# One five-bank PSUM tile for the scores of two attention units, one maximum and one exponential per unit

## The chip, the cores and the metric

The kernel runs on one core of a Trainium2 chip. The metric is the device time of one execution in microseconds, as the median of several runs.

## The reference

A two-layer backbone over 1024 latent tokens and 256 context tokens with a model width of 1024. Each layer normalises its input, makes one combined projection, feeds three groups of heads (gated DeltaNet, latent attention, GLA), gates them and makes one output projection. Context reads only context, latent tokens read all 1280. The change touches the attention of the latent head group:

```python
def attend(q, k, v):
    s = jnp.einsum('bqhd,bkhd->bhqk', q, k).astype(jnp.float32) * MLA_SCALE
    p = jax.nn.softmax(s, axis=-1).astype(v.dtype)
    return jnp.einsum('bhqk,bkhd->bqhd', p, v)

o_l = blocked_attention(q_l, concat([k_c, k_l]), concat([v_c, v_l]))   # 8 heads, 1024 queries, 1280 keys
o_c = attend(mla_q(cq_c, ...), k_c, v_c)                               # 256 queries, 256 keys, first layer only
```

## The kernel before, in words

Each layer runs in stages: projections, preparation of the DeltaNet, the up-projections of attention (`up`, L1014), attention (`attend`, L1134) and the output projection. The two recurrent scans run in the background: `background` (L1453) is a generator that goes through the DeltaNet scan (`gdn_scan`, 20 steps, two or three yields each), then the GLA preparation, seven GLA levels (`gla_level`) and the GLA scan. `up` takes its first 28 steps. In `run`, the loop at L1481 calls the background's next step after each yield of `attend`, so yields fix how the two are mixed in the order of the program. The framework turns that into a fixed order of instructions for each engine, which need not be the program's, and puts in the waits.

`attend` goes through units. A unit is one head and 128 queries (at i < CT, 256 context queries against 256 keys, done as two halves of 128). Two heads `hh` and two query tiles make a group of four units, and four pairs of heads `m` make 64 units of the large kind in each layer, and 8 of the context kind in the first. A unit goes through these steps:

- `first(u, c0)` (L1190) makes the scores of the keys 0 to 511 and 512 to 1023 into `sa`, a tile of two PSUM banks with two buffers. Each piece is three matmuls (`mm3`, L253 to L257, from high and low halves of queries and keys). After the second piece VectorE takes the negated maximum over 1024 keys (L1206).
- `second(u)` (L1208) makes the scores of the last 256 keys into half of `sb`, a tile of one bank that two following units share (L1222 to L1224), takes their maximum (L1225), the smaller of the two negated maxima (L1226), and then two exponentials on ScalarE with that bias, 256 keys from `sb` (L1227) and 1024 from `sa` (L1228), each with a sum into `rd`. They write the tile `P`, which has three buffers.
- `transposed(u, ka)` (L1230) turns P in pieces of 128 keys on TensorE, four to a bank of the tag `t` (two buffers), and copies them to `PT`: the first and last piece on ScalarE, the middle one on VectorE (L1247).
- `output(m, i)` (L1250) runs once for the four units of a group: 20 pairs of value and PT through TensorE into the tile `O` (L1255), the two sums added (L1261) and inverted (L1262), a diagonal of them multiplied in (L1267), and the gate (L1269, L1271).

The loop from L1278 sets the order of the program. In step u it issues `second(u)`, then three times a part of `transposed(u - 1)` and, at the first two of them, a part of `first(u + 1)`, with a yield after each, and `output` where a group has ended. That makes six yields a unit, and one more for an output. PSUM is full: `sa` 4 banks, `sb` 1, `t` 2, and 1 for the background (tag `l`).

Of the kernel before, what the change touches and what calls it, by code (L numbers as in the profile page):

```python
# [9 lines left out]
F32 = mybir.dt.float32  # L10
F32R = mybir.dt.float32r
U32 = mybir.dt.uint32
AF = mybir.ActivationFunctionType
ALU = mybir.AluOpType
AX = mybir.AxisListType
# [4 lines left out]
T = 1280  # L20
CT = 2
# [22 lines left out]
class Net:  # L44
# [1089 lines left out]
    def attend(self, l, fill=None):  # L1134
        nc, sp = self.nc, self.ap
        last = l == L - 1
        mm = nc.tensor.matmul
        V, A, P = nc.vector, nc.scalar, nc.gpsimd
# [34 lines left out]
        sb, mxs, sas, ps, PT, rds = {}, {}, {}, {}, {}, {}  # L1173
# [16 lines left out]
        def first(u, c0):  # L1190

            m, i, hh = units[u]
            if i < CT:
                if c0 == 0:
                    sas[u] = sa = self.ps.tile([128, 1024], F32, name="sa", tag="sa", bufs=2)[:, 0:512]
                    for j in range(2):
                        scores(u, sa[:, 256 * j:256 * j + 256], 0, 256, j)
                    mxs[u] = mx = sp.tile([128, 2], F32, name="mx", tag="mx", bufs=4)
                    V.tensor_reduce(mx, sa.rearrange("p (j k) -> p j k", j=2), AX.X, ALU.max, negate=True)
                return  # L1200
            if c0 == 0:
                sas[u] = self.ps.tile([128, 1024], F32, name="sa", tag="sa", bufs=2)
            scores(u, sas[u][:, c0:c0 + 512], c0, 512)
            if c0 == 512:
                mxs[u] = mx = sp.tile([128, 2], F32, name="mx", tag="mx", bufs=4)
                V.tensor_reduce(mx[:, 0:1], sas[u], AX.X, ALU.max, negate=True)  # L1206

        def second(u):  # L1208

            m, i, hh = units[u]  # L1210
            mx, ta = mxs.pop(u), sas.pop(u)
            if hh == 0 and i % 2 == 0:
                rds[m, i] = sp.tile([128, 2, 2, 2], F32, name="rd", tag="rd", bufs=3)
            r = rds[m, i - i % 2][:, hh, i % 2, :]
            ps[u] = p = self.ab.tile([128, T], F32, name="P", tag="P", bufs=PB)
            if i < CT:
                for j in range(2):
                    J = slice(256 * j, 256 * j + 256)
                    A.activation(p[:, J], ta[:, J], AF.Exp, bias=mx[:, j:j + 1], accum_out=r[:, j:j + 1])
                return  # L1220
            if u // 2 not in sb:
                sb[u // 2] = self.ps.tile([128, 512], F32, name="sb", tag="sb", bufs=1)  # L1222
            tb = sb[u // 2][:, 256 * (u % 2):256 * (u % 2) + 256]
            scores(u, tb, 1024, 256)  # L1224
            V.tensor_reduce(mx[:, 1:2], tb, AX.X, ALU.max, negate=True)  # L1225
            V.tensor_tensor(mx[:, 0:1], mx[:, 0:1], mx[:, 1:2], ALU.min)  # L1226
            A.activation(p[:, 1024:T], tb, AF.Exp, bias=mx[:, 0:1], accum_out=r[:, 1:2])  # L1227
            A.activation(p[:, 0:1024], ta, AF.Exp, bias=mx[:, 0:1], accum_out=r[:, 0:1])  # L1228
# [21 lines left out]
        def output(m, i):  # L1250
# [7 lines left out]
            if i < CT:  # L1258
                V.reciprocal(ri, rd[:, :, 0, :])
            else:  # L1260
                V.tensor_tensor(ri, rd[:, :, :, 0], rd[:, :, :, 1], ALU.add)  # L1261
                V.reciprocal(ri, ri)  # L1262
# [13 lines left out]
        first(0, 0)  # L1276
        first(0, 512)
        for u in range(n + 1):  # L1278
# [5 lines left out]
            for x in range(3):  # L1284
                if u > 0:
                    transposed(u - 1, 4 * x)
                    yield
                if u + 1 < n and x < 2:
                    first(u + 1, 512 * x)
                    yield  # L1290
# [293 lines left out]
```

## Time and profile before

| what | us |
|---|---|
| median of 3 runs | 2279.19 |
| lowest and highest run | 2273.74, 2281.04 |
| the profiled execution | 2280.18 |
| its span, first to last instruction | 2278.4 |
| TensorE busy (PE) | 2043.3, 90% |
| VectorE busy (DVE) | 1291.6, 57% |
| ScalarE busy (ACT) | 941.1, 41% |

Busy times are of the one profiled execution. PE is the matmul stream of TensorE and PEld its weight loads, which overlap. Attention stands between 625 and 1065 us in the first layer and between 1755 and 2165 us in the second. A wait is named by the instruction that ended it. An activation with a sum shows as two rows, the activation and ACTIVATION_READ_ACCUMULATOR.

### The profile page before, as it was taken

The numbers are of one execution on the slowest core, as the hardware profiler recorded it, in microseconds if no ns is written. First come the engines' busy times: TensorE is split into PE (matmuls) and PEld (weight loads), VectorE is DVE, ScalarE is ACT, GpSimd is POOL, SyncE is SP. The second block draws the span as 40 slices with busy tenths as digits, with TensorE's granted clock in tenths as the row PEclk, the third lists the DMA queues.
The fourth block names the chain that finished last, engine by engine and source line by source line (L and its number), as shares of the span: only waits on it lengthen the run. The fifth ranks groups of instructions, "written<-read, shape, count | busy, mean of one in ns | idle before, by whom it ended". The sixth has DMA issues, their size and how long they took to land.

```text
span 2278.4 us, 44490 instructions
## 1 busy us (share of the span) xinstructions
PE 2043.3 (90%) x17820; PEld 1709.8 (75%) x17820; DVE 1291.6 (57%) x2187; ACT 941.1 (41%) x1926; POOL 743.7 (33%) x936
## 2 busy tenths in 40 slices
PE   5998997999989988898897998976987999899998
PEld 3987896886767766676897987875876776667688
DVE  3446685323447689656425356795233677975634
ACT  3246311533235466555204356212542445564531
POOL 1233265122234543214103322381123264421410
PEclk8999998899989999999898999998998999899999
DMA  7111343258742231113424212424266242101352
GB/s 296 47 62 61 105 119 113 84 200 284 220 109 76 76 111 36 40 48 121 161 93 171 65 36 81 136 69 115 90 197 168 58 115 96 54 24 50 100 155 103
DMA packets 207551, 247.34 MB, mean 109 GB/s; under 512 B 60976, under 2 KB 164464, under 8 KB 203760
## 3 DMA queue, kind: packets, MB, share of 16 engines
q1 hardware_dynamic: 207344, 244.49, 34.1%
q8 instruction: 140, 2.29, 0.4%
q14 instruction: 67, 0.55, 0.1%
HBM read 168.14 MB, written 76.28 MB: 107 GB/s over the span
## 4 chain that ended last, share of the span: by engine, by line
PE 46%; DVE 13%; ACT 5%; DMA 5%; issue 3%; POOL 2%; SPq 1%; DVEq 0%; POOLq 0%; ACTq 0%
PE O L1255 6%; PE ptr L1243 4%; PE po L257 3%; PE po L255 3%; PE po L256 3%; PE sa L255 3%; PE sa L256 2%; PE sa L257 2%; PE ptk L255 1%; PE ptk L256 1%; PE ptk L257 1%; DVE XT L634 1%; DVE X L636 1%; PE kS L730 1%; DVE acc L345 1%
## 5 line engine op out<-in xcount | busy, mean ns | idle before, releaser
L255 PE MATMUL ptk<-whi,hhi 128*128 128x256 f32 (+1 forms) x912 | 263.6, 290 | 6.1 <-DVE ev L297 2.2
L257 PE MATMUL ptk<-whi,hlo 128*128 128x256 f32 (+1 forms) x912 | 261.9, 288 | 1.8 <-POOL hlo L238 1.7
L256 PE MATMUL ptk<-wlo,hhi 128*128 128x256 f32 (+1 forms) x912 | 261.7, 287 | 0.4 <-DVE wlo L250 0.4
L1243 PE MATMUL ptr<-c_id,P 128*128 128x128 f32 x1312 | 203.6, 283 | 27.8 <-ACT PT L1247 18.8
L1243 PEld LDWEIGHTS ptr<-c_id,P 128*128 128x128 f32 x1312 | 151.2, 143 | 78.1 <-ACT PT L1247 29.9
L1247 ACT COPY PT<-ptr 128x512 f32<-128x512 f32 (+1 forms) x256 | 122.3, 480 | 211.1 <-PE ptr L1243 209.7
L256 PE MATMUL pin<-hlo,whi 128*128 128x512 f32 (+1 forms) x544 | 201.6, 371 | 1.6 <-issue 1.6
L255 PE MATMUL pin<-hhi,whi 128*128 128x512 f32 (+1 forms) x544 | 202.5, 372 | 0.0
L257 PE MATMUL pin<-hhi,wlo 128*128 128x512 f32 (+1 forms) x544 | 201.8, 372 | 0.0
L255 PEld LDWEIGHTS ptk<-whi,hhi 128*128 128x128 f32 x912 | 179.4, 197 | 10.8 <-issue 4.3
L1206 DVE TENSOR_REDUCE mx<-sa 128x1 f32<-128x1024 f32 x128 | 156.2, 1220 | 53.6 <-PE sa L257 53.0
L257 PEld LDWEIGHTS ptk<-whi,hlo 128*128 128x128 f32 x912 | 178.8, 197 | 5.3 <-POOL hlo L238 3.0
L256 PEld LDWEIGHTS ptk<-wlo,hhi 128*128 128x128 f32 x912 | 179.4, 197 | 3.1 <-issue 2.0
L1255 PE MATMUL O<-PT,vv 128*64 128x256 f32 x1312 | 169.6, 388 | 1.7 <-ACT PT L1247 0.9
L255 PE MATMUL po<-wohi,yh 128*128 128x256 f32 x576 | 164.4, 286 | 4.4 <-DVE yl L1353 2.1
L256 PE MATMUL po<-wolo,yh 128*128 128x256 f32 x576 | 164.0, 285 | 0.0
L257 PE MATMUL po<-wohi,yl 128*128 128x256 f32 x576 | 162.6, 285 | 0.0
L1228 ACT ACTIVATE P<-sa,mx 128x1024 f32<-128x1024 f32 x128 | 142.2, 1111 | 0.0
L1255 PEld LDWEIGHTS O<-PT,vv 128*64 128x64 f32 x1312 | 97.2, 138 | 59.0 <-issue 11.9
L255 PE MATMUL sa<-kTh,qTh 128*128 128x512 f32 (+1 forms) x272 | 118.3, 436 | 21.1 <-ACT kTh L1152 15.2
L250 POOL TENSOR_TENSOR wlo<-wst,whi 128x1024 fp32r<-128x1024 f32 x32 | 84.1, 2639 | 127.5 <-ACT whi L249 126.4
L256 PEld LDWEIGHTS pin<-hlo,whi 128*128 128x128 f32 x544 | 105.6, 194 | 19.7 <-issue 4.4
(341 smaller groups left out, 5030.6 us busy)
## 6 DMA issues: line engine op xcount, KB each, us to landing
wada<-in_w_ada_dram SPq DMA_DIRECT2D x24, 1024.0 KB
wst<-in_w_in_dram SPq DMA_DIRECT2D x48, 512.0 KB
kv<-ktv_d SPq DMA_DIRECT2D x80, 128.0 KB
wost<-in_w_out_dram SPq DMA_DIRECT2D x16, 512.0 KB
xt<-in_x_all_dram SPq DMA_DIRECT2D x10, 512.0 KB
at_d<-D SPq DMA_DIRECT2D x4, 1280.0 KB
kn_d<-uo SPq DMA_DIRECT2D x20, 256.0 KB
v_d<-uo SPq DMA_DIRECT2D x20, 256.0 KB
```

Source lines behind the costliest of these rows:

```text
L250: E.tensor_tensor(lo[:, h], st, hi[:, h].bitcast(F32), ALU.subtract)
L255: mm(out, lh, rh, start=first, stop=False)
L256: mm(out, lh, rl, start=False, stop=False)
L257: mm(out, ll, rh, start=False, stop=last)
L345: nc.vector.scalar_tensor_tensor(a, raw[:, tap:tap + 1282], cw[:, ti, tap:tap + 1], a, ALU.mult, ALU.add)
L634: E.tensor_tensor(tmp, Xv[B, G, 0:k, k].unsqueeze(3).broadcast_to([q, n, nr, ncl]), Xv[B, G, k, k + 1:32].unsqueeze(2).broadcast_to([q, n, ...
L636: E.tensor_tensor(dst, dst, tmp, ALU.add)
L1206: V.tensor_reduce(mx[:, 0:1], sas[u], AX.X, ALU.max, negate=True)
L1228: A.activation(p[:, 0:1024], ta, AF.Exp, bias=mx[:, 0:1], accum_out=r[:, 0:1])
L1243: nc.tensor.transpose(tp[:, 128 * (k - ka):128 * (k - ka) + 128], p[:, 128 * c:128 * c + 128], self.ident)
L1247: (V.tensor_copy if ka == 4 else A.copy)(PT[hh][:, ka:kb, 128 * (i % 2):128 * (i % 2) + 128], tp[:, 0:128 * (kb - ka)].rearrange("p (k t) ...
L1255: mm(po[64 * h2:64 * h2 + 64, 0:256], vv[m][:, 128 * k + 64 * h2:128 * k + 64 * h2 + 64], PT[h2][:, k, :], start=(k == 0), stop=(k == nk - 1))
```

## The change

`sa` and `sb` go. One tile `both` of 2560 columns (five banks) is made once; even units use columns 0 to 1279 (banks 0, 1 and half of 2), odd units 1280 to 2559 (the other half of bank 2, banks 3 and 4). All scores of a unit are made in `first`, in three pieces that each stay in one bank: 512, 512 and 256 keys for even units, 256, 512 and 512 for odd ones. After the third there is one maximum over 1280 keys. `second` is left with one exponential over 1280 keys and one sum, and `output` with the reciprocal alone. The loop calls `first` at all three places and so yields seven times a unit.

```diff
--- before.py
+++ after.py
@@ -1170,7 +1170,15 @@
 
         groups = [(m, i) for m in range(4) for i in range(lt0, NT, 2)]
         units = [(m, i + j, hh) for m, i in groups for hh in range(2) for j in range(1 if i < CT else 2)]
-        sb, mxs, sas, ps, PT, rds = {}, {}, {}, {}, {}, {}
+        mxs, ps, PT, rds = {}, {}, {}, {}
+        both = self.ps.tile([128, 2 * T], F32, name="sc", tag="sc", bufs=1)
+
+        def room(u):
+
+            return both[:, T * (u % 2):T * (u % 2) + T]
+
+        def pieces(u):
+            return (((0, 512), (512, 512), (1024, 256)), ((0, 256), (256, 512), (768, 512)))[u % 2]
 
         def scores(u, dst, c0, cn, j=0):
             m, i, hh = units[u]
@@ -1187,45 +1195,37 @@
                 if (m, i - i % 2) not in qTs:
                     load_q(m, i - i % 2)
 
-        def first(u, c0):
+        def first(u, x):
 
             m, i, hh = units[u]
+            S = room(u)
             if i < CT:
-                if c0 == 0:
-                    sas[u] = sa = self.ps.tile([128, 1024], F32, name="sa", tag="sa", bufs=2)[:, 0:512]
+                if x == 0:
                     for j in range(2):
-                        scores(u, sa[:, 256 * j:256 * j + 256], 0, 256, j)
+                        scores(u, S[:, 256 * j:256 * j + 256], 0, 256, j)
                     mxs[u] = mx = sp.tile([128, 2], F32, name="mx", tag="mx", bufs=4)
-                    V.tensor_reduce(mx, sa.rearrange("p (j k) -> p j k", j=2), AX.X, ALU.max, negate=True)
+                    V.tensor_reduce(mx, S[:, 0:512].rearrange("p (j k) -> p j k", j=2), AX.X, ALU.max, negate=True)
                 return
-            if c0 == 0:
-                sas[u] = self.ps.tile([128, 1024], F32, name="sa", tag="sa", bufs=2)
-            scores(u, sas[u][:, c0:c0 + 512], c0, 512)
-            if c0 == 512:
+            c0, cn = pieces(u)[x]
+            scores(u, S[:, c0:c0 + cn], c0, cn)
+            if x == 2:
                 mxs[u] = mx = sp.tile([128, 2], F32, name="mx", tag="mx", bufs=4)
-                V.tensor_reduce(mx[:, 0:1], sas[u], AX.X, ALU.max, negate=True)
+                V.tensor_reduce(mx[:, 0:1], S, AX.X, ALU.max, negate=True)
 
         def second(u):
 
             m, i, hh = units[u]
-            mx, ta = mxs.pop(u), sas.pop(u)
+            mx, S = mxs.pop(u), room(u)
             if hh == 0 and i % 2 == 0:
-                rds[m, i] = sp.tile([128, 2, 2, 2], F32, name="rd", tag="rd", bufs=3)
-            r = rds[m, i - i % 2][:, hh, i % 2, :]
+                rds[m, i] = sp.tile([128, 2, 2], F32, name="rd", tag="rd", bufs=3)
+            r = rds[m, i - i % 2][:, hh]
             ps[u] = p = self.ab.tile([128, T], F32, name="P", tag="P", bufs=PB)
             if i < CT:
                 for j in range(2):
                     J = slice(256 * j, 256 * j + 256)
-                    A.activation(p[:, J], ta[:, J], AF.Exp, bias=mx[:, j:j + 1], accum_out=r[:, j:j + 1])
+                    A.activation(p[:, J], S[:, J], AF.Exp, bias=mx[:, j:j + 1], accum_out=r[:, j:j + 1])
                 return
-            if u // 2 not in sb:
-                sb[u // 2] = self.ps.tile([128, 512], F32, name="sb", tag="sb", bufs=1)
-            tb = sb[u // 2][:, 256 * (u % 2):256 * (u % 2) + 256]
-            scores(u, tb, 1024, 256)
-            V.tensor_reduce(mx[:, 1:2], tb, AX.X, ALU.max, negate=True)
-            V.tensor_tensor(mx[:, 0:1], mx[:, 0:1], mx[:, 1:2], ALU.min)
-            A.activation(p[:, 1024:T], tb, AF.Exp, bias=mx[:, 0:1], accum_out=r[:, 1:2])
-            A.activation(p[:, 0:1024], ta, AF.Exp, bias=mx[:, 0:1], accum_out=r[:, 0:1])
+            A.activation(p, S, AF.Exp, bias=mx[:, 0:1], accum_out=r[:, i % 2:i % 2 + 1])
 
         def transposed(u, ka):
             m, i, hh = units[u]
@@ -1255,11 +1255,7 @@
                     mm(po[64 * h2:64 * h2 + 64, 0:256], vv[m][:, 128 * k + 64 * h2:128 * k + 64 * h2 + 64],
                        PT[h2][:, k, :], start=(k == 0), stop=(k == nk - 1))
             ri = sp.tile([128, 2, 2], F32, name="ri", tag="ri", bufs=2)
-            if i < CT:
-                V.reciprocal(ri, rd[:, :, 0, :])
-            else:
-                V.tensor_tensor(ri, rd[:, :, :, 0], rd[:, :, :, 1], ALU.add)
-                V.reciprocal(ri, ri)
+            V.reciprocal(ri, rd)
             for h2 in range(2):
                 dg = sp.tile([128, 256], F32, name="dg", tag="dg", bufs=2)
                 for x in range(2):
@@ -1273,8 +1269,8 @@
 
         n = len(units)
         prepare(0)
-        first(0, 0)
-        first(0, 512)
+        for x in range(3):
+            first(0, x)
         for u in range(n + 1):
             if u + 1 < n:
                 prepare(u + 1)
@@ -1285,8 +1281,8 @@
                 if u > 0:
                     transposed(u - 1, 4 * x)
                     yield
-                if u + 1 < n and x < 2:
-                    first(u + 1, 512 * x)
+                if u + 1 < n:
+                    first(u + 1, x)
                     yield
             if u > 0 and (u == n or units[u][0:2] not in (units[u - 1][0:2], (units[u - 1][0], units[u - 1][1] + 1 - 2 * (units[u - 1][1] % 2)))):
                 output(units[u - 1][0], units[u - 1][1] - units[u - 1][1] % 2)
```

## Rows read from the trace of the kernel before

**Rows 1.** The page: busy time by engine, and the granted clock in 40 slices
```profile
PE 2043.3 (90%) x17820; PEld 1709.8 (75%) x17820; DVE 1291.6 (57%) x2187; ACT 941.1 (41%) x1926; POOL 743.7 (33%) x936
PEclk8999998899989999999898999998998999899999
```

**Rows 2.** Windows: us, then busy us of PE, PEld, DVE, ACT, POOL; clock, DMA share, GB/s
```profile
650.00:800.00 150.00, 147.39 (x1537) 112.10 (x1537) 101.39 (x207) 76.09 (x181) 66.61 (x90) 1.00 0.26 75
800.00:975.00 175.00, 152.40 (x1385) 107.38 (x1382) 142.70 (x249) 108.85 (x252) 65.09 (x82) 0.95 0.19 58
1775.00:1925.00 150.00, 147.84 (x1599) 114.36 (x1598) 105.42 (x210) 72.20 (x169) 66.99 (x88) 1.00 0.28 80
1925.00:2050.00 125.00, 106.21 (x995) 80.01 (x996) 107.22 (x181) 78.94 (x175) 44.96 (x56) 0.89 0.18 55
```

**Rows 3.** Instructions of the tile mx: ns min/median/max, first and last start
```profile
L1206 DVE TENSOR_REDUCE mx<-sa x128: 1185/1224/1227, 648.8 to 2149.1; 128x1 f32<-128x1024 f32 x128
L1225 DVE TENSOR_REDUCE mx<-sb x128: 385/414/425, 649.9 to 2155.3; 128x1 f32<-128x256 f32 x128
L1226 DVE TENSOR_TENSOR mx<-mx x128: 128/159/1819, 651.0 to 2155.7; 128x1 f32<-128x1 f32 x128
L1227 ACT ACTIVATE P<-sb,mx x128: 460/479/521, 651.5 to 2157.5; 128x256 f32<-128x256 f32 x128
L1227 ACT ACTIVATION_READ_ACCUMULATOR P<-sb,mx x128: 185/202/247, 651.8 to 2157.9; 128x1 f32 x128
L1228 ACT ACTIVATE P<-sa,mx x128: 1089/1114/1161, 651.9 to 2158.0; 128x1024 f32<-128x1024 f32 x128
```

**Rows 4.** Groups by line, L1261: busy us, mean ns, idle before it
```profile
L1261 DVE TENSOR_TENSOR ri<-rd 128x4 f32<-128x4 f32 x32 | 8.4, 264 | 4.9 <-ACT P L1228 4.4
```

**Rows 5.** Counts by line: L754, L1228 in 650:775; L1225 in 800:975, in 1925:2050
```profile
L754 DVE TENSOR_TENSOR Sg<-sd,F x9: 406/410/422, 658.2 to 767.3; 128x256 f32<-128x256 f32 x9
L1228 ACT ACTIVATE P<-sa,mx x23: 1104/1114/1118, 651.9 to 774.4; 128x1024 f32<-128x1024 f32 x23
L1225 DVE TENSOR_REDUCE mx<-sb x22: 401/416/425, 801.9 to 962.9; 128x1 f32<-128x256 f32 x22
L1225 DVE TENSOR_REDUCE mx<-sb x17: 406/414/425, 1930.2 to 2045.8; 128x1 f32<-128x256 f32 x17
```

**Rows 6.** Timeline about 906 and 1045 us: start us, us, instruction, idle before it
```profile
1045.06 0.20 ACT L1227 ACTIVATION_READ_ACCUMULATOR P<-sb,mx 128x1 f32 x1
1045.32 0.39 PE L255 MATMUL sb<-kTh,qTh 128*128 128x256 f32 x1
...
906.65 0.19 ACT L1227 ACTIVATION_READ_ACCUMULATOR P<-sb,mx 128x1 f32 x1
906.90 0.38 PE L255 MATMUL sb<-kTh,qTh 128*128 128x256 f32 x1 [0.96 <-ACT P L1227]
907.24 0.28 PE L257 MATMUL sb<-kTh,qTl 128*128 128x256 f32 x1
907.56 0.42 DVE L1225 TENSOR_REDUCE mx<-sb 128x1 f32<-128x256 f32 x1 [0.43 <-PE sb L257]
```

**Rows 7.** Timeline, 1851 to 1876 us, first score matmul into sb of each unit
```profile
1851.70 0.36 PE L255 MATMUL sb<-kTh,qTh 128*128 128x256 f32 x1
...
1857.01 0.36 PE L255 MATMUL sb<-kTh,qTh 128*128 128x256 f32 x1
...
1861.41 0.36 PE L255 MATMUL sb<-kTh,qTh 128*128 128x256 f32 x1
...
1871.32 0.36 PE L255 MATMUL sb<-kTh,qTh 128*128 128x256 f32 x1
...
1875.72 0.36 PE L255 MATMUL sb<-kTh,qTh 128*128 128x256 f32 x1
```

**Rows 8.** Waits of PE over the whole run: us, times, longest
```profile
PE sb L255 <- ACT P L1227: 11.3, 8, 2.7
```

**Rows 9.** Timeline about 1044 us, the ten transposes of a unit
```profile
1044.00 1.50 PE L1243 MATMUL ptr<-c_id,P 128*128 128x128 f32 x10
```

## The prediction, made before the changed kernel ran

> **What bounds the kernel now.** I read the page first, then the attention stages by windows, then the single instructions and the timeline. The page gives TensorE 2043.3 us of 2278.4 and VectorE only 1291.6, at a clock that is mostly full [rows 1]. The change touches attention alone, so its stages decide. The windows show two kinds [rows 2]. In 650 to 800 and 1775 to 1925 us, where the DeltaNet scan runs beside attention, TensorE is busy 147.4 and 147.8 of 150 us at clock 1.00: it is the bound, and relief of VectorE or ScalarE is worth nothing there. In 800 to 975 and 1925 to 2050 us, where the GLA levels run beside it, TensorE is busy 152.4 of 175 and 106.2 of 125 us, at clocks 0.95 and 0.89, and VectorE is busy 82% and 86%. There VectorE sets much of the pace. The change adds no matmul and takes none away, so it can gain only in this second kind of stage, and lose in both.
>
> **What is removed.** Of VectorE a unit now takes a maximum over 1024 keys (1224 ns), one over 256 (414 ns) and a minimum (159 ns), medians of one shape each [rows 3]: 1797 ns. The new maximum reads 1280 keys. From the two sizes an element costs (1224 - 414)/768 = 1.055 ns, so 1280 take 1224 + 256 x 1.055 = 1494 ns. That saves 303 ns. The addition of the two sums at L1261, 264 ns once in four units [rows 4], saves 66 ns more: **0.37 us of VectorE per unit**, 47 us over 128 units. On ScalarE the two exponentials take 479 and 1114 ns [rows 3]; one over 1280 takes by the same slope 1114 + 256 x 0.827 = 1326 ns, which saves **0.27 us per unit**. One accumulator read of 202 ns goes too; it lies beside the next activation, so I count nothing for it; the next activation covers it, and if it didn't, it would be a gain of 0.2 us.
>
> **What is moved.** The scores of the last 256 keys were issued in second(u), just ahead of their own maximum; now they are the third piece of first(u + 1), one step earlier. Their matmuls are the same in number and size: 0 us of TensorE. No DMA and no queue moves, and the five banks are those that sa and sb had, so no other tile loses one. The step now yields seven times, not six, to the background, which would put the scans further ahead in program order. I cost this at nothing, because the order of issue is not the program's: in 650 to 775 us the trace has 9 steps of the scan against 23 units [rows 5], though program order at six yields a unit and three a step asks for two steps a unit. The scan runs as its own results allow. What hides the seventh yield is that lag; without it, background work would come earlier and attention later, with the total of TensorE unchanged. The few instructions at the start and end of each layer's attention swap a short for a long maximum, below 1 us a layer either way.
>
> **What is added: a new wait.** Bank 2 of the five holds the last 256 keys of an even unit and the first 256 of an odd one. Does writing one half wait for the readers of the other? Today's sb is shared just so. The score matmul at 1045.32 us is the 62nd of its layer, the second half of its tile, and starts 0.06 us after the accumulator read of the other half's exponential ended at 1045.26; so does the one at 906.90, which opens a new tile [rows 6]. In the timeline none of the 126 that follow another in their layer starts before that. So halves of a bank are kept apart.
> The Trainium skill, in "PSUM — Partial Sum Buffer", section Terms, says why it must be so: two engines on one bank and quadrant at once raise an error, so their accesses have to be serialised; this speaks against the change. By that rule, the trace agrees, every unit carries the loop below, and the sum is the one below; with independent halves the loss of 3 us in it would go.
>
> The loop per unit is: score piece in bank 2, maximum, exponential, next unit's piece in bank 2. Today it is short: matmuls from 906.90 to 907.52, 0.62 us, 0.04 to the maximum [rows 6], then 0.41 + 0.16 + 0.48, about 0.2 for the accumulator's end and the hops (an estimate from the 0.04 and 0.06 seen): 1.9 us. In the changed kernel it is 0.62 + 0.04 + 1.49 + 1.33 + 0.2 = **3.7 us**. Behind the waiting piece on TensorE queue the other matmuls of attention and of the scans; behind those wait the PT copies of ScalarE and VectorE and the scan's next products; and on ScalarE the copy of the older unit's transposes sits behind the longer exponential. Does 3.7 us fit? In the scan stages the sb groups start at 1851.70, 1857.01, 1861.41, 1871.32 and 1875.72 [rows 7]: 5.3, 4.4, 9.9 and 4.4 us apart, the 9.9 with an output in it. The shortest leaves 0.7 us for queues on VectorE and ScalarE, and the one with the output 6. The two free score pieces of the next unit and the older unit's transposes don't need bank 2 and can go ahead. So there I cost it at 0, hidden by that TensorE work; if the cover were gone the bound is in the slow rival.
> In the GLA stages the loop is already late at times: over the whole run TensorE waits 11.3 us in 8 waits for L1227 before sb [rows 8]. Each could grow by the 1.8 us that the loop gains, 14 us in all, or by none, since one long VectorE instruction now queues where three did. Nothing shown lies between; I take 3 us, near the lower end, because [rows 7] show the piece usually arriving late on TensorE for other reasons.
>
> **The sum.** 22 units fall in 800 to 975 us and 17 in 1925 to 2050 [rows 5]. I credit VectorE's 0.37 us by the share of time in which VectorE is busy [rows 2]: 0.37 x (22 x 0.82 + 17 x 0.86) = 12 us. Bounds: 0, if the scans' own latency sets these stages, and 39 x (0.37 + 0.27) = 25 us if both engines' relief counts in full. ScalarE (109 of 175 us, 79 of 125) is no bound, so I give it 0 in the sum. Then -12 + 3 = -9 us. The profiled execution took 2280.18 us (span 2278.4 and 1.8 around it), so 2271 for it; the median of the runs, 2279.19, is 1 us lower: **2270 us**, with its own range 2254 to 2273. By a measurement's worth, about 0.3% or 6.8 us, this counts as faster.
>
> **The rivals.**
> *No change.* The relief falls into time in which VectorE waits for the scan's results or for TensorE, which holds the bound in the stages of the first kind anyway, and the bank costs a few us: between -6 and +6, 2279 us. For it: even in the GLA stages VectorE is idle 14 to 18%. Against it: TensorE is not the bound there, and what is left is VectorE or what waits on it.
> *Slower by the shared bank.* Place: the piece in bank 2. It decides once queues add more than 0.7 us to the 3.7, since the 4.4 us intervals are then too short. With 1.2 us the loop is 4.9 and two intervals in four lose 0.5 each, 1 us per four units; at 24.0 us per four units [rows 7] the 300 us of the scan stages hold 12.5 such periods, some 13 us. In the GLA stages, if every second of 39 units waits the 1.8 us more, 35 us. Less the 12 us of relief: +36, 2315 us. For it: both engines run in order, and the PT copies and the scans' products stand ahead of the loop's instruction. Against: free work is there to put ahead.
> *It doesn't do what it says.* If the one tile of five banks were tracked as a whole, all score pieces would wait for the exponential of the unit before. Then only the ten transposes (1.50 us in a row [rows 9]) cover 1.49 + 1.33 + 0.2 us, TensorE idles 1.5 us in each of 128 units, and the time is near 2279 + 195 = 2474 us. The trace has no tile of several banks with a reader of some of them, so it can't be excluded; separate banks of one tile need no such wait.
>
> **How the numbers follow.** Forecast, relief with a hidden loop: 0.42. No change: 0.25. Slower by the bank: 0.30. Whole tile: 0.03. Faster by over 0.3% is then 0.42, within it 0.25, slower 0.33. The range runs from the full relief of both engines, 2279 - 25 = 2254, rounded to 2253, up to the slow rival's 2315; the whole-tile case, and a third of the slow rival's, with queues longer than 1.2 us, stay outside: 0.13. As cases of both signs hold most of the chance, the forecast's own range stands above.
>
> **What would show it.** Right: L1206's successor near 1.49 us and one activation near 1.33; in the GLA windows VectorE's busy time lower, and these windows shorter by some 5 us a layer; in the scan windows TensorE still above 98% busy; waits of the score piece for the exponential below 15 us in the whole run. Wrong by the loop: these waits at 30 us or more, TensorE below 96% in the scan windows, score pieces of bank 2 starting 0.06 us after the exponential's accumulator read in most units. Wrong by the whole tile: first score pieces in banks 0, 1, 3 and 4 waiting as well. Wrong by the relief: VectorE's busy time lower but the GLA windows as long as before.

## The result, and the profile after

| | before | after |
|---|---|---|
| median of 4 runs, us | 2279.16 | 2340.41 |
| lowest and highest, us | 2273.74, 2281.04 | 2338.22, 2341.22 |
| the profiled execution, us | 2280.18 | 2341.03 |
| its span, us | 2278.4 | 2339.2 |

After stands to before as 1.0271 (95% interval 1.0252 to 1.029): the change costs 61 us. The prediction, 2270 us, had the wrong sign, and its range ended at 2315.

The page of the changed kernel, engines, and the groups of the new tile `sc` and of what reads it (columns: busy us, mean ns, idle before and what ended most of it):

```profile
PE 2058.7 (88%) x17820; PEld 1716.3 (73%) x17820; DVE 1247.4 (53%) x1899; ACT 916.8 (39%) x1670; POOL 745.0 (32%) x936
...
L1213 DVE TENSOR_REDUCE mx<-sc 128x1 f32<-128x1280 f32 x128 | 190.7, 1490 | 170.2 <-PE sc L257 166.0
...
L255 PE MATMUL sc<-kTh,qTh 128*128 128x512 f32 (+1 forms) x400 | 165.7, 414 | 54.9 <-ACT P L1228 33.6
...
L1228 ACT ACTIVATE P<-sc,mx 128x1280 f32<-128x1280 f32 x128 | 170.0, 1328 | 106.4 <-DVE mx L1213 106.0
```

Beside [rows 1], VectorE has 44.2 us less to do and ScalarE 24.3, with the same 17820 matmuls. The merged instructions take 1490 and 1328 ns. VectorE's saving is close to the 47 us forecast, ScalarE's is 24 of the 35 that 0.27 us in each of 128 units make, and the kernel is slower. TensorE's idle time in the span went from 2278.4 - 2043.3 = 235.1 to 280.5 us; that is 45 of the 61 us, and the other 15 are its busy time, which rose by 15.4 us at a mean granted clock of 0.941 instead of 0.946.

The windows of [rows 2], now of the changed kernel (same columns):

```profile
650.00:800.00 150.00, 135.55 (x1409) 102.52 (x1409) 84.16 (x132) 60.32 (x110) 62.13 (x85) 0.95 0.25 69
800.00:975.00 175.00, 144.85 (x1316) 105.50 (x1315) 127.24 (x191) 97.47 (x192) 56.05 (x74) 0.92 0.18 56
1775.00:1925.00 150.00, 127.71 (x1446) 99.20 (x1445) 72.92 (x123) 53.24 (x89) 58.80 (x75) 0.93 0.38 104
1925.00:2050.00 125.00, 102.86 (x1104) 75.87 (x1104) 96.61 (x138) 67.72 (x122) 58.31 (x68) 0.95 0.22 69
```

The two stages in which TensorE was full have lost most: 135.6 us busy instead of 147.4, and 127.7 instead of 147.8 (the second layer starts 41 us later, so its windows hold another part of the stage). The GLA stage of the first layer, where the gain was to come, lost 7.6 us of TensorE time as well.

What holds up the scores is seen in the timeline, three units late in the first layer, where the loop is bare (start us, us, instruction, idle before):

```profile
1026.66 1.49 DVE L1213 TENSOR_REDUCE mx<-sc 128x1 f32<-128x1280 f32 x1 [3.69 <-PE sc L257]
...
1028.19 1.33 ACT L1228 ACTIVATE P<-sc,mx 128x1280 f32<-128x1280 f32 x1 [2.68 <-DVE mx L1213]
...
1029.41 0.19 ACT L1228 ACTIVATION_READ_ACCUMULATOR P<-sc,mx 128x1 f32 x1
...
1029.66 0.50 PE L255 MATMUL sc<-kTh,qTh 128*128 128x512 f32 x1
...
1031.40 0.28 PE L257 MATMUL sc<-kTh,qTl 128*128 128x256 f32 x1
...
1031.78 1.49 DVE L1213 TENSOR_REDUCE mx<-sc 128x1 f32<-128x1280 f32 x1 [1.34 <-PE sc L257]
...
1033.31 1.33 ACT L1228 ACTIVATE P<-sc,mx 128x1280 f32<-128x1280 f32 x1 [0.57 <-DVE mx L1213]
...
1034.54 0.19 ACT L1228 ACTIVATION_READ_ACCUMULATOR P<-sc,mx 128x1 f32 x1
...
1034.78 0.39 PE L255 MATMUL sc<-kTh,qTh 128*128 128x256 f32 x1
...
1036.91 1.49 DVE L1213 TENSOR_REDUCE mx<-sc 128x1 f32<-128x1280 f32 x1 [1.21 <-PE sc L257]
```

Follow it down. The read of one unit's sums ends at 1029.60; at 1029.66 the next, an even unit, begins with 512 keys, in bank 0. The odd unit before it lies in banks 2 to 4, so the two do not meet in bank 0. All three pieces wait, and not only the one in bank 2. Two maxima are 2.12 (all scores) + 1.53 (maximum) + 1.42 (exponential and its sums) + 0.05 = 5.12 us apart, and the next two 5.13. Over the 126 pairs of following units no first piece begins before the exponential of the unit before has ended, and 59 begin 0.04 to 0.06 us after it. The shortest distance of two maxima is 5.05 us in either layer; before it was 1.47 in the first and 2.00 in the second. The median of the first layer went from 5.11 to 5.93 us and the whole, first maximum to last, from 404.2 to 457.6 us in the first layer and from 383.7 to 424.1 in the second.

That is 53 + 40 = 94 us of attention for 61 us of time. Where the rest went is read from the last step of the GLA scan (L980) and attention's last output (L1255), first of the kernel before, then of the changed one (first and last start, first layer):

```profile
L980 PE MATMUL gF<-gvt,ktl x36: 377/379/483, 960.7 to 1046.6; 128*128 128x256 f32 x36
...
L1255 PE MATMUL O<-PT,vv x672: 379/379/690, 649.8 to 1074.1; 128*64 128x256 f32 x168
```

```profile
L980 PE MATMUL gF<-gvt,ktl x36: 377/378/454, 961.9 to 1060.0; 128*128 128x256 f32 x36
...
L1255 PE MATMUL O<-PT,vv x672: 379/379/689, 652.9 to 1125.4; 128*64 128x256 f32 x168
```

Attention before thus runs to 1074 us, some 9 past the 1065 given above. The scans end only 13 us later: they took the TensorE time that attention left. Attention then stands by itself for 65 us instead of 28, and its last output is 51 us late. The second layer's scan (L759) starts at 1749.9 instead of 1708.8 us, 41 late: the output projection and what follows gave 10 back. In the second layer the last maximum is 79 us late and the end 61, so 18 are given back there.

### The profile page after: what moved, and what is told of

The parts are those of the page before. It is cut to its first block, busy times and chain, and to the rows that moved or that the text cites. A ratio compares the mean times of both kernels' runs of the same rounds, so it can differ in the third digit from the quotient of the medians.

```text
span 2339.2 us, 43940 instructions
## 1 busy us (share of the span) xinstructions
PE 2058.7 (88%) x17820; PEld 1716.3 (73%) x17820; DVE 1247.4 (53%) x1899; ACT 916.8 (39%) x1670; POOL 745.0 (32%) x936
## 5 line engine op out<-in xcount | busy, mean ns | idle before, releaser
L1213 DVE TENSOR_REDUCE mx<-sc 128x1 f32<-128x1280 f32 x128 | 190.7, 1490 | 170.2 <-PE sc L257 166.0
L255 PE MATMUL sc<-kTh,qTh 128*128 128x512 f32 (+1 forms) x400 | 165.7, 414 | 54.9 <-ACT P L1228 33.6
L1228 ACT ACTIVATE P<-sc,mx 128x1280 f32<-128x1280 f32 x128 | 170.0, 1328 | 106.4 <-DVE mx L1213 106.0
L1255 PE MATMUL O<-PT,vv 128*64 128x256 f32 x1312 | 169.7, 385 | 7.1 <-ACT PT L1247 5.0
L256 PE MATMUL sc<-kTl,qTh 128*128 128x512 f32 (+1 forms) x400 | 150.1, 375 | 3.5 <-POOL kTl L1153 3.5
L257 PE MATMUL sc<-kTh,qTl 128*128 128x512 f32 (+1 forms) x400 | 149.6, 374 | 0.0
L255 PEld LDWEIGHTS sc<-kTh,qTh 128*128 128x128 f32 x400 | 80.7, 202 | 88.8 <-ACT P L1228 46.7
```

What stands on the lines that cost most here:

```text
L255: mm(out, lh, rh, start=first, stop=False)
L256: mm(out, lh, rl, start=False, stop=False)
L257: mm(out, ll, rh, start=False, stop=last)
L1213: V.tensor_reduce(mx[:, 0:1], S, AX.X, ALU.max, negate=True)
L1228: A.activation(p, S, AF.Exp, bias=mx[:, 0:1], accum_out=r[:, i % 2:i % 2 + 1])
L1255: mm(po[64 * h2:64 * h2 + 64, 0:256], vv[m][:, 128 * k + 64 * h2:128 * k + 64 * h2 + 64], PT[h2][:, k, :], start=(k == 0), stop=(k == nk - 1))
```

## The experiments

Theory: the framework keeps the tile `sc` apart as a whole (it lets no engine write any part of it while another reads any part), so a unit's scores wait for the exponential of the unit before, whatever banks the two use. Rivals: the wait comes from bank 2 alone; the loss comes from the moved piece and the seventh yield; the merged instructions themselves cost. Each run is set against runs of the kernel before on the same chip. No run leaves work out; four add a reduction whose result nothing uses. Diffs are shown in part, with `...` where lines are left out.

**Before's instructions in one tile.** Two maxima and two exponentials as before, every tile in the bank that it had, only cut from one five-bank tile:

```diff
+        both = self.ps.tile([128, 2560], F32, name="sc", tag="sc", bufs=1)
+
+        def room(u):
+            return both[:, 1536 * (u % 2):1536 * (u % 2) + 1024]
...
-                sas[u] = self.ps.tile([128, 1024], F32, name="sa", tag="sa", bufs=2)
+                sas[u] = room(u)
...
-                sb[u // 2] = self.ps.tile([128, 512], F32, name="sb", tag="sb", bufs=1)
+                sb[u // 2] = both[:, 1024:1536]
```

> The kernel before, instruction for instruction, with sa and sb laid into one five-bank tile (even units banks 0 and 1, odd units banks 3 and 4, the shared piece in bank 2), so that every instruction touches the banks it touched. If a tile is kept apart as a whole between engines, every score piece waits for the exponential of the unit before, and the shared piece for the maximum over the other two banks as well: the loop of a unit becomes 1.4 (two pieces) + 1.22 + 0.62 + 0.41 + 0.16 + 0.48 + 1.2 and some 0.4 of hops, near 5.9 us, longer than the 5.1 us seen in the changed kernel: 2370 to 2440 us. If banks are kept apart singly, nothing changes: 2279 within 7 us.

Measured 2577.58 us, ratio 1.1314 (1.1285 to 1.1343). Two units meet only in bank 2, as in the kernel before, and yet (timeline of this run):

```profile
1053.57 1.10 ACT L1233 ACTIVATE P<-sc,mx 128x1024 f32<-128x1024 f32 x1
1054.56 0.20 ACT L1233 ACTIVATION_READ_ACCUMULATOR P<-sc,mx 128x1 f32 x1
1054.82 0.80 PE L255 MATMUL sc<-kTh,qTh 128*128 128x512 f32 x1 [2.25 <-ACT P L1233]
...
1057.85 1.22 DVE L1211 TENSOR_REDUCE mx<-sc 128x1 f32<-128x1024 f32 x1 [4.84 <-PE sc L257]
...
1059.13 0.58 PE L255 MATMUL sc<-kTh,qTh 128*128 128x256 f32 x1
```

The piece of 512 keys at 1054.82, in the banks that the older unit does not use, starts 0.06 us after that unit's exponential has ended; 86 of 126 start 0.04 to 0.06 us after it and none earlier. The 256-key piece at 1059.13 begins 0.06 us after the end of a maximum that reads two other banks, and none of the 128 begins before its unit's maximum has ended. The tile is kept apart as a whole: this is shown, with no merged instruction in it. The shortest distance of maxima is 6.07 us, near the 5.9 expected, but the median of the first layer is 8.40; a unit goes through the tile twice here, one wait after another, and why most units take so much longer than the shortest was not taken apart. The loss is thus far larger than expected (2440 at most). It needs no merged instruction; whether these add to it is taken up below.

Every reader so far covers several banks. The context units answer for a reader of a single one: their exponentials read 256 columns each, all in bank 0 for an even unit, and the odd unit after it begins in bank 2. In the changed attention that stands alone (2833.45 us, below) it waits all the same: in three of the four pairs it begins 0.05 us after the sums, in the fourth later (timeline):

```profile
1017.57 0.20 ACT L1226 ACTIVATION_READ_ACCUMULATOR P<-sc,mx 128x1 f32 x1
...
1017.82 0.38 PE L255 MATMUL sc<-kTh,qTh 128*128 128x256 f32 x1 [0.81 <-ACT P L1226]
```

**Bank 2 last.** The changed kernel, odd units making their piece in bank 2 third instead of first:

```diff
-            return (((0, 512), (512, 512), (1024, 256)), ((0, 256), (256, 512), (768, 512)))[u % 2]
+            return (((0, 512), (512, 512), (1024, 256)), ((256, 512), (768, 512), (0, 256)))[u % 2]
```

> The changed kernel with the pieces of odd units in another order, the one in bank 2 last, as it already is for even units. If banks are kept apart singly, two of three pieces of every unit are now free to go ahead of the exponential, the loop falls to 3.7 us and the time to 2265 to 2300 us. If the whole tile is kept apart, all three pieces still wait, the loop stays at 5.1 us and the time at 2340 within 7 us.

Measured 2342.36 us, ratio 1.0281 (1.0258 to 1.0304), the changed kernel's own time. An odd unit here (timeline):

```profile
1028.32 0.20 ACT L1228 ACTIVATION_READ_ACCUMULATOR P<-sc,mx 128x1 f32 x1
1028.57 0.50 PE L255 MATMUL sc<-kTh,qTh 128*128 128x512 f32 x1
...
1029.37 0.39 PE L255 MATMUL sc<-kTh,qTh 128*128 128x512 f32 x1
...
1030.07 0.28 PE L255 MATMUL sc<-kTh,qTh 128*128 128x256 f32 x1
```

Its first 512 keys still start only after the sums, at 0.05 us, and the shortest distance of maxima stays 5.04 us. Bank 2 alone is not what is waited for.

**The maximum taken twice**, to load the suspected loop (and VectorE with it):

```diff
+                V.tensor_reduce(mx[:, 1:2], S, AX.X, ALU.max, negate=True)
                 V.tensor_reduce(mx[:, 0:1], S, AX.X, ALU.max, negate=True)
```

> The changed kernel with the maximum over 1280 keys taken twice, the first into a column that nobody reads. If the loop through the tile sets the pace, 1.5 us more in each of 128 units shows for the most part, since the loop is the floor of most units: 2440 to 2530 us. If only VectorE's load counts, by the share of its busy time in the stages of the GLA levels, it is 1.5 x 33 units, 50 us: 2375 to 2400 us.

Measured 2518.22 us, ratio 1.1066 (1.1031 to 1.11): 178 us above the changed kernel, 1.39 us a unit. The added instruction takes 1480 ns (its group):

```profile
L1214 DVE TENSOR_REDUCE mx<-sc 128x1 f32<-128x1280 f32 x128 | 189.4, 1480 | 0.0
```

Of 1.48 us put into the loop, 94% reach the end of the kernel. The sum alone can't tell the loop from VectorE's load, but the place can: attention's last output of the first layer comes 84 us later than in the changed kernel (1209.1 against 1125.4 us), the last step of the GLA scan 15 us later (1075.4 against 1060.0). It is attention that the loop holds back.

**VectorE loaded outside the loop.** The kernel before with one more reduction a unit whose result is not used, first of a constant, then of the unit's own P, 256 and 1024 columns:

```diff
             V.tensor_tensor(mx[:, 0:1], mx[:, 0:1], mx[:, 1:2], ALU.min)
+            V.tensor_reduce(sp.tile([128, 1], F32, name="jk", tag="jk", bufs=2), self.bdm, AX.X, ALU.max)
```

```diff
             A.activation(p[:, 0:1024], ta, AF.Exp, bias=mx[:, 0:1], accum_out=r[:, 0:1])
+            V.tensor_reduce(sp.tile([128, 1], F32, name="jk", tag="jk", bufs=2), p[:, 0:256], AX.X, ALU.max)
```

> The kernel before with one more VectorE reduction in each unit, 256 columns of a constant into a column that nobody reads, with no wait on either side, near 0.4 us each. It measures what VectorE's time is worth, the credit of the prediction with the sign turned. If the credit by VectorE's busy share in the stages of the GLA levels holds: 0.4 x 33, 10 to 16 us slower. If VectorE's time is not what sets these stages: within 5 us.

> The kernel before with one more VectorE reduction a unit, over 256 columns of the unit's own P, so that it can't run ahead of its unit as the one over a constant did; nothing uses its result, and it stands after the exponentials, outside the chain of scores, maximum and exponential. About 0.4 us of VectorE a unit, the size of what the merge saves (0.37 us). If my credit by VectorE's busy share holds: 0.4 x (22 x 0.82 + 17 x 0.86) = 13 us, 2292 us, ratio 1.0057. If VectorE's time in attention is worth nothing: within 0.2% of before.

> The same with 1024 columns, about 1.2 us of VectorE a unit. If the credit by busy share holds and is linear: about 39 us, 2318 us, ratio 1.017; if VectorE's time in the scan stages counts as well: over 60 us. If VectorE has room enough: within 0.5% of before.

| added | median us | ratio | interval |
|---|---|---|---|
| 0.41 us, of a constant | 2279.05 | 0.9989 | 0.9974 to 1.0004 |
| 0.41 us, of P | 2283.0 | 1.0015 | 1.0 to 1.0029 |
| 1.21 us, of P | 2366.71 | 1.0394 | 1.0366 to 1.0421 |

The first says nothing. Its reductions wait for no unit, and all ran in two bursts at the start of attention (616 to 651 and 1740 to 1780 us), as the tile's first and last start show; in the second run they are spread over both layers:

```profile
L1227 DVE TENSOR_REDUCE jk<-c_bdm x128: 401/408/416, 616.3 to 1779.6; 128x1 f32<-128x256 f32 x128
```

```profile
L1229 DVE TENSOR_REDUCE jk<-P x128: 396/414/421, 658.4 to 2164.7; 128x1 f32<-128x256 f32 x128
```

There 0.41 us a unit, more than the 0.37 that the merge saves, costs 3 us (0 to 6.6), where my credit asked for 13. Three times as much costs 90 us (0.0394 x 2280), not three times 3: the expectation's case of over 60 us came, and not the straight line. It falls on the scans and not on attention: in the first layer their last step is 24 us late (1071.1 against 1046.6 us) and attention's last output 7 (1081.3 against 1074.1), the other way round than with the maximum taken twice. VectorE has some room beside attention, and little beyond it. By this measure the relief is worth a few us; that taking 0.4 us off is worth no more than putting 0.4 us on costs was not tried.

**The move alone.** Before's tiles, maxima and exponentials; the last 256 keys and their maximum go into `first` as its third piece, and the step yields seven times:

```diff
-                if u + 1 < n and x < 2:
+                if u + 1 < n:
                     first(u + 1, 512 * x)
                     yield
```

> The kernel before with its own tiles, two maxima and two exponentials, but with the score piece of the last 256 keys, its maximum and the minimum moved into the third part of first and with the seventh yield. If the move and the yield cost nothing, as the prediction had it: 2279 within 8 us. If the denser background is part of the loss: 2290 us or more.

Measured 2280.2 us, ratio 0.9999 (0.9984 to 1.0013). The moved piece and the seventh yield cost nothing in the kernel before, and that rival falls.

**The maximum split.** In the changed kernel the first two pieces get a maximum of their own, ahead of the third:

```diff
+            if x == 1:
...
+                V.tensor_reduce(mx[:, 0:1], S[:, 0:c0 + cn], AX.X, ALU.max, negate=True)
             if x == 2:
...
+                V.tensor_reduce(mx[:, 1:2], S[:, c0:T], AX.X, ALU.max, negate=True)
+                V.tensor_tensor(mx[:, 0:1], mx[:, 0:1], mx[:, 1:2], ALU.min)
```

> The changed kernel with the maximum split: one over the first two pieces, one over the third, and a minimum, so that the first could run beside the third piece's matmuls; the one exponential stays. With single banks the even units' loop shrinks by up to 0.9 us, since their third piece lies in another bank than the first two: 2300 to 2335 us. With the whole tile the third piece has to wait for the first maximum, the loop of even units is 1.4 + 1.22 + 0.6 + 0.41 + 0.16 + 1.33 and some 0.35 of hops, 5.5 us against 5.1: 2345 to 2390 us.

Measured 2561.87 us, ratio 1.1247 (1.1225 to 1.1269), slower as the whole tile asks, but far outside both ranges. What was meant to shorten the loop made it longer, since the third piece now waits for the first maximum (timeline of an odd unit, whose maximum reads 768 keys of banks 2 and 3 and whose third piece goes to bank 4):

```profile
1036.55 0.96 DVE L1213 TENSOR_REDUCE mx<-sc 128x1 f32<-128x768 f32 x1 [4.67 <-PE sc L257]
...
1037.58 0.48 PE L255 MATMUL sc<-kTh,qTh 128*128 128x512 f32 x1
```

The piece begins 0.07 us after the maximum has ended, and none of the 128 begins before its unit's. TensorE's wait for the exponential in all, in the changed kernel and here (us, times, longest):

```profile
PE sc L255 <- ACT P L1228: 33.6, 42, 2.2
```

```profile
PE sc L255 <- ACT P L1232: 154.3, 83, 5.1
```

That each wait within the loop also lets other work of the three engines go ahead, and so costs more than its own length, fits these waits and those of the first experiment, but no run takes it apart.

**Own tiles.** The clean cure, a tile for each unit, needs six banks; beside the background's one only one is left for the transposes. All units make their pieces as 512, 512 and 256 keys. The control is the kernel before with that same loss:

```diff
-        both = self.ps.tile([128, 2 * T], F32, name="sc", tag="sc", bufs=1)
...
+                rooms[u] = self.ps.tile([128, 1536], F32, name="sc", tag="sc", bufs=2)[:, 0:T]
...
-                self.ps, self.psb = self.pool(st, "psB", space=PSUM), {"t": 2}
+                self.ps, self.psb = self.pool(st, "psB", space=PSUM), {"t": 1}
```

> The changed kernel with a three-bank tile for each unit in two buffers in place of the one five-bank tile; the sixth bank is taken from the tag t, which keeps one buffer. One maximum and one exponential stay. If the loss comes from the shared tile, it goes: the score pieces of a unit wait for the exponential of the unit two before, and the time is that of the kernel before with one t buffer (run e4) less at most the relief of 12 to 25 us that was forecast. If the loss comes from the longer maximum and exponential themselves or the seventh yield, it is 40 us or more above e4.

> The kernel before with one buffer for the tag t in place of two, as the control for the run with a tile for each unit. Transposes, their copies and the output then take turns in one bank. No theory disagrees here; slower than before, 2290 to 2380 us.

Measured 2630.7 us, ratio 1.1534 (1.15 to 1.1569), and for the control 2569.59 us, 1.1283 (1.1253 to 1.1314). One bank for the transposes costs 290 us by itself, far more than expected. The merged form was 61 us slower even so, and by the bound set beforehand (40 us above the control) the merged instructions have a cost of their own, besides that of the tile. Whether that holds where transposes have two banks this pair can't say. I tried next to free a bank.

**The background first.** In the order of the program the background runs to its end ahead of attention, and its pool is closed before attention's opens; done to the kernel before, to own tiles (two banks for the transposes), and to the changed kernel:

```diff
+            for _ in bg:
+                pass
+            sq.close()
...
                 for _ in self.attend(l):
-                    if bg is not None and next(bg, bg) is bg:
-                        bg = None
-                for _ in bg or ():
                     pass
```

> The kernel before with the background scans run to their end before attention starts, so that attention has TensorE, VectorE and ScalarE to itself and the background's PSUM bank is free. Control for the next two. Slower than before by the time in which the scans now run alone, 300 to 700 us; TensorE busy above 95% in attention, four units in some 19 to 20 us.

> The changed kernel in that order, with a three-bank tile of its own for each unit (two buffers, six banks) and both buffers of t, which the free bank now allows. One maximum and one exponential over 1280 keys stay, the shared tile is gone. If the shared tile is the whole loss: within 10 us of f1 or up to 20 us faster. If the longer maximum and exponential are themselves part of the loss, as the pair of runs with one t buffer left open: 30 us or more slower than f1.

> The changed kernel in that order, with its five-bank tile. Every unit's loop of 5.1 us (all scores 2.1, maximum 1.5, exponential 1.3, hops 0.2) stands against some 4.9 us of TensorE work per unit, and an output of 6 us in every fourth unit can't make up for it, since it is done while the loop waits or not at all: 40 to 120 us slower than f1. If the tile costs nothing without the background: within 10 us of f1.

| run | median us | ratio | interval |
|---|---|---|---|
| before's attention | 2271.08 | 0.9956 | 0.9943 to 0.9969 |
| own tiles | 2661.55 | 1.1653 | 1.1616 to 1.1691 |
| the changed attention | 2340.58 | 1.0254 | 1.0226 to 1.0282 |

The first expectation was wrong in an instructive way: attention still overlaps the background, since it takes seven banks and the background's eighth stays its own; the order of the program decides little. That version beats both kernels, by 0.44% of the one before (10 runs); why this order is a little better was not looked into. With the changed attention in that order the shortest distance of maxima is again 5.04 us, and the loss against it 69.5 us. Own tiles take the eighth bank, so attention really waits for the background there (first large maximum at 922 us), and the run can't be set against the other two.

**Attention alone.** So I gave the others eight banks too: before's attention and the changed one with three banks for the transposes (`{"t": 3}`), then before's with two, and a bank of `sb` for each unit:

```diff
-                sb[u // 2] = self.ps.tile([128, 512], F32, name="sb", tag="sb", bufs=1)
-            tb = sb[u // 2][:, 256 * (u % 2):256 * (u % 2) + 256]
+            tb = self.ps.tile([128, 512], F32, name="sb", tag="sb", bufs=2)[:, 0:256]
```

> Before's instructions and tiles in attention (two maxima, two exponentials), the background run to its end first, and three banks for the transposes, so that all eight banks are taken and attention stands alone, as it did in f2_own_alone (2661.55 us). If the merged maximum and exponential are worth nothing where the tiles are apart and TensorE sets the pace (what e8_idle_reduce says of VectorE's time): within 15 us of f2_own_alone, median spacing of the maxima in attention about 4.0 us. If the 0.37 us of VectorE and 0.27 us of ScalarE a unit count in full: 47 to 82 us above f2_own_alone.

> The changed kernel's attention (one five-bank tile) in the same order, three banks for the transposes, attention alone. If the loop through the whole tile is what costs: no spacing of two maxima below 5.0 us, and 60 to 140 us above g1_before_serial and f2_own_alone (5.1 against 4.0 us in 128 units, 141 us, if the outputs cover none of it). If the loss of the changed kernel came from the work beside attention instead, it falls away here: within 15 us of f2_own_alone.

> Before's two maxima and two exponentials, background first, two banks for the transposes, and the last 256 keys of every unit in a bank of its own (two banks for sb): eight banks taken, no tile shared by two units, so it stands against f2_own_alone (2661.55 us, merged, spacing of maxima 4.0 us) with nothing else different. If the merged instructions themselves slow an attention that stands alone, this runs 40 to 80 us faster than f2_own_alone, with a median spacing near the 2.9 us of g1_before_serial (2594.94 us). If the third bank for the transposes made that difference instead, it lies within 15 us of f2_own_alone, spacing near 4.0 us.

| attention alone | median us | ratio | interval | median between maxima, first layer |
|---|---|---|---|---|
| before, three banks for transposes | 2594.94 | 1.1366 | 1.1327 to 1.1405 | 3.06 |
| before, own `sb`, two banks | 2631.83 | 1.153 | 1.1506 to 1.1554 | 4.34 |
| merged, own tiles, two banks | 2661.55 | 1.1653 | 1.1616 to 1.1691 | 4.03 |
| merged, one shared tile, three banks | 2833.45 | 1.2437 | 1.2374 to 1.2501 | 6.04 |

The last two lines against the first two bear on two things. With nothing beside attention the change costs 2833.45 - 2594.94 = 239 us, 1.9 us a unit, more than I had expected and four times the 61 us of the changed kernel. Of that at least 2833.45 - 2661.55 = 172 us is the shared tile, since own tiles with the same merged instructions, and one bank less for the transposes, take 2661.55. So the loss does not come from the work beside attention; that work hides about three quarters of it. TensorE's waits in the run with the shared tile, with own tiles, and with before's instructions on two banks:

```profile
PE sc L255 <- ACT P L1228: 166.6, 98, 5.5
```

```profile
PE sc L255 <- ACT P L1230: 36.2, 56, 1.4
```

```profile
PE sa L255 <- ACT P L1226: 20.4, 43, 0.5
```

And the merge gains nothing with tiles apart: 2661.55 against 2631.83 us, same banks for the transposes, intervals that do not meet. Both of my expectations for that run missed, since each named one cause and there are two: the third bank is worth some 37 us, and 30 us stand against the merge. Not all of these 30 are its own. The two profiled executions are 25 us apart; attention, from its first score to its last output, is 3.9 us longer in the first layer and 11.5 in the second, and 6.6 lie ahead of the first score, where both do the same work (granted clock 0.93 against 1.00 in 500 to 600 us). So the merge costs some 15 us in attention. The pair also differs in where the last 256 keys stand, which cost nothing in the kernel before. The rows suggest why a merge can cost. From the last score to the end of the exponentials the merged unit needs 1.49 + 1.33 = 2.82 us; the old one 0.41 + 0.16 + 0.48 + 1.11 = 2.16 [rows 3], because its long maximum runs beside the third piece. That this is the cause was only argued.

## Why the prediction was wrong, step by step

**The step that failed: the new wait.** "The two free score pieces of the next unit and the older unit's transposes don't need bank 2 and can go ahead. So there I cost it at 0". The score pieces cannot go ahead: the tile is kept apart, not the bank. The term put at 0 is the loss of 61 us. The loop holds all three pieces, 2.1 us, not the one of 0.62, and is 5.1 us instead of 3.7. The prediction's own test says what that means: against intervals of 4.4 us [rows 7] a loop of 3.7 fits and one of 5.1 does not. How much of the 61 us the merged instructions add by themselves stays open: they cost 61 us where the transposes had one bank and some 15 where attention stood alone, and own tiles beside the scans, with two banks for the transposes, would need nine banks.

**The reading behind it.** I took [rows 6] as proof that halves of a bank are kept apart. But `sb` is a tile of one bank, so those rows could not tell the bank from the tile. The two readings agree on the old kernel and part on the new one. On the page "PSUM — Partial Sum Buffer" of the Trainium skill, section Terms, two engines on one bank and quadrant at once are an error; that rule speaks of single banks and does not ask for the waits that the first experiment shows between different ones. No run here shows the error itself.

**The rival that was right and cheap.** "If the one tile of five banks were tracked as a whole, all score pieces would wait for the exponential of the unit before" is what happened. It had 0.03, because "separate banks of one tile need no such wait"; need is not what the framework goes by. Its price, 195 us, was the idle time of TensorE if nothing else filled it; with attention alone the change costs 239, and beside the scans, which fill it, 61. Mechanism and price were both in the text; what was missing was the scans as cover.

**The relief of 12 us.** "I credit VectorE's 0.37 us by the share of time in which VectorE is busy" was too large, as far as an added load can show it: the same amount, added beside the loop, costs 3 us, and the cost then grows much faster than the load. A busy share of 82% in a window is no price for a microsecond.

**What held.** The durations, 1494 and 1326 ns against 1490 and 1328, and with them VectorE's saving, 44 us of the 47. The moved piece and the seventh yield at 0, by the run of the move alone. In 650 to 775 us the scan again takes 9 steps, while only 17 units pass instead of 23 [rows 5]. Of the signs named, "TensorE below 96% in the scan windows" (90% and 85%), the waits of 30 us or more (33.6) and the first pieces waiting as well all came.

## What to carry to other kernels

Before two users share one tile, ask by what unit the framework tracks it, and look for a trace in which that unit and the physical one differ; a tile of one bank cannot tell. Where the tile is the unit, two buffers cut from one tile work as one buffer. A first price for time saved on an engine comes from an extra instruction of that size in the old kernel, made to depend on the work beside which it is to stand; an instruction that depends on nothing can run elsewhere and price nothing.

## What was not expected of the hardware

A much slower attention also lost some clock: the mean granted clock was 0.91 in the first experiment (2577.58 us), and 0.859 where before's attention stood alone (2594.94 us), where runs of the kernel before lie between 0.939 and 0.956. The changed kernel's 0.941 to 0.945 lie within that. The window of 700 to 915 us of that last run, where the scans run without attention (columns as in [rows 2]):

```profile
700.00:915.00 215.00, 122.13 (x979) 85.94 (x976) 100.69 (x192) 52.96 (x117) 53.91 (x64) 0.51 0.12 39
```

TensorE is busy 57% of it, and the granted clock of 0.51 lies at the lower of its two levels, 1.2 GHz. Before it fell, TensorE was busy 94.0 of 100 us at a clock of 1.00 (500 to 600 us), then 34.7 of 50 at 0.74 and 29.9 of 50 at 0.50. The clock is a part of why the runs with attention alone are so long, a part that no run measures; over the span it is alike in those compared with each other (0.858, 0.859 and 0.861, and 0.847 in the slowest).

The second surprise is the order: with the background finished first in the program, attention and the scans overlapped as before, and the time was 0.44% lower. Only where attention took the eighth bank did it wait for the scans.
